# A gather kernel: loading a third block of one batch's rows ahead, in four pieces issued between ScalarE's zeroing copies

**Chip, cores, metric.** One core of a Trainium2 chip. The metric is the time of one execution on the device in microseconds (us); lower is better. Times are medians. A ratio is the mean time of one kernel's fast runs over the mean of the other's fast runs of the same rounds, so it is not quite the ratio of the medians quoted. A run is called fast or slow by how far it lies from the fastest of the same kernel.

## The reference

```python
# x: (32, 512, 1024) float32; indices: (32, 128) int32 in 0..511, drawn with a fixed seed
for b in range(batch):
    result[b] = x[b, indices[b]]          # (128, 1024) per batch
```

It is a gather of 128 rows of 4 KB from each of 32 batches. Among 128 draws from 512 rows there are repeats: a batch names 109 to 120 distinct rows. The kernel uses that.

## The kernel before

Batches 0 to 4 (the HEAD) are gathered straight by their index columns, repeats included. For every later batch the kernel works out which positions are the first to name a row, gathers only those rows into one of eight ring buffers `u` (places that are not needed get an index out of bounds and are skipped: in the profile of this kernel the gather queue moved 15.01 MB, where 32 x 128 whole rows would be 16.78), and then spreads the rows to all 128 positions with a 0/1 matrix on TensorE. ScalarE copies the product from PSUM, and SyncE stores the block. The ring buffers are zeroed once by ScalarE, so that a skipped place holds zeros.

Batch 5 (HALF) is treated specially: rows 0 to 255 of it are loaded as two plain blocks at the start, before any index is known, and only its rows from 256 up are gathered. These are the parts concerned, with cuts marked:

```python
early = [rows.tile([N, D], F32, name=f"early{k}") for k in range(2)]
for k in range(2):                                    # ScalarE's DMA queue
    load = act(nc.scalar.dma_start, out=early[k][:], in_=xf[HALF * S + k * N:HALF * S + (k + 1) * N])
# ... indices transposed; then the head:
for b in range(HEAD):
    gather(blocks[b], ..., b)                         # GpSimd, indirect DMA
    store(b)                                          # SyncE, 512 KB to DRAM
# ... in step0 of batch 5's group: a row below 2N counts as already present
#         scalar=2.0 * N, in1=cnt[:, c], op0=ALU.is_lt, op1=ALU.add
held = []
for k in range(RING):
    u = ring.tile([N, D], F32, name=f"u{k}")
    act(nc.scalar.copy, out=u[:], in_=zero[:].to_broadcast([N, D]))
    held.append(u)
# ... half_rows(h, last=False): product of the early blocks, kept open in PSUM
#         for k in range(2):
#             pe(mm, ps[:], lhsT=spread[HALF, "early"][k], rhs=early[k][:, w], start=k == 0, stop=False)
step0(0); step0(1)
for g in range(AHEAD):                                # groups of three batches
    step1(g)                                          # TensorE, VectorE: place of each row
    if 0 < g < AHEAD - 1: step0(g + 1)
    step2(g)                                          # the rows to gather and the spread matrix
    for b in of_group(g):
        if b < HEAD + RING: fetch(b)                  # GpSimd gathers into the ring
    if g == 0: half_spread()
    elif g < 3: half_rows(g - 1, False)
for b in range(HEAD, B):
    spread_rows(b); fetch(b + RING)                   # product, copy, store; next gather
    # ... steps of a later group
```

On TensorE the early products of batch 5 stand between the steps that yield the addresses of groups 1, 2 and 3: the gathers of a later group are not issued before TensorE has come through the products ahead of their step.

Of the kernel before, what the change touches and what calls it, by code (L numbers as in the profile page):

```python
# [6 lines left out]
F32 = mybir.dt.float32  # L7
# [21 lines left out]
def kernel(ctx, tc, x, indices, out):  # L29
# [16 lines left out]
    nc = tc.nc  # L46
    B, S, D = x.shape
    N = indices.shape[1]
    HEAD, RING, GROUP, AHEAD, FAR = 5, 8, 3, 4, 1024
    HALF = HEAD  # L50
    PAIRED = range(12, 20)
    GROUPS = (B - HEAD) // GROUP
    assert 2 * N <= S <= FAR and (B - HEAD) % GROUP == 0
    const = ctx.enter_context(tc.tile_pool(name="const", bufs=1))
    ring = ctx.enter_context(tc.tile_pool(name="ring", bufs=1))
    rows = ctx.enter_context(tc.tile_pool(name="rows", bufs=1))
    pick = ctx.enter_context(tc.tile_pool(name="pick", bufs=1))
# [5 lines left out]
    pe, dve, act = InOrder(tc), InOrder(tc), InOrder(tc)  # L63
    mm, v = nc.tensor.matmul, nc.vector
# [12 lines left out]
    for p0, p1, at0 in ((0, 36, 0), (36, 48, 112), (48, 104, 36), (104, 108, 124), (108, N, 92)):  # L77
# [16 lines left out]
        in_=vals[:].bitcast(I32).rearrange("p (n two) -> p n two", two=2)[:, :, 0])  # L94
# [2 lines left out]


    xf = x.flatten_outer_dims()
    early = [rows.tile([N, D], F32, name=f"early{k}") for k in range(2)]  # L100
    for k in range(2):
        load = act(nc.scalar.dma_start, out=early[k][:], in_=xf[HALF * S + k * N:HALF * S + (k + 1) * N])
        if k == 0:
# [9 lines left out]
    idxF = const.tile([N, B], F32, name="idxF")  # L113
# [14 lines left out]
    for b in range(B):  # L128
        if b not in PAIRED:
            blocks[b] = rows.tile([N, D], F32, name=f"block{b}")[:]  # L130
# [5 lines left out]
    def store(b):  # L136
        if b not in PAIRED:
            nc.sync.dma_start(out=of[b * N:(b + 1) * N], in_=blocks[b])
        elif b % 2:
            nc.sync.dma_start(out=of[(b - 1) * N:(b + 1) * N].rearrange("(t p) d -> p t d", t=2),  # L140
                              in_=blocks[b - 1, "pair"][:])
# [5 lines left out]
    def table(name, dtype):  # L147
        return const.tile([N, B], dtype, name=name)

    cnt, lead, slot = table("cnt", F32), table("lead", F16), table("slot", F16)  # L150
# [4 lines left out]
    bcs, packs, spread = {}, {}, {}  # L155

    def of_group(g):
        return range(HEAD + g * GROUP, HEAD + (g + 1) * GROUP)

    def cols(t, g):  # L160
        return t[:, HEAD + g * GROUP:HEAD + (g + 1) * GROUP]
# [4 lines left out]
    def step0(g):  # L166

        bcs[g] = bc = pbc.tile([N, 4, N], F32, name="bc")
        for k, b in enumerate(of_group(g)):
            pe(mm, bc[:, k], lhsT=ident[:, b:b + 1].to_broadcast([N, N]), rhs=vf[:], start=True, stop=True)  # L170
        for k, b in enumerate(of_group(g)):
            junk = junkp.tile([N, N], F16, name="junk")
            dve(v.scalar_tensor_tensor, out=junk[:], in0=bc[:, k], scalar=idxF[:, b:b + 1], in1=below[:],
                op0=ALU.is_equal, op1=ALU.mult, accum_out=cnt[:, b:b + 1])
        if HALF in of_group(g):
            c = slice(HALF, HALF + 1)
            dve(v.scalar_tensor_tensor, out=cnt[:, c], in0=idxF[:, c], scalar=2.0 * N, in1=cnt[:, c],
                op0=ALU.is_lt, op1=ALU.add)
        dve(v.tensor_scalar, out=cols(lead, g), in0=cols(cnt, g), scalar1=0.0, scalar2=None, op0=ALU.is_equal)
        for b in of_group(g):  # L180
            if b < B - 2:
                dve(v.tensor_tensor, out=past[:, b + 1:b + 2], in0=past[:, b:b + 1], in1=lead[:, b:b + 1], op=ALU.add)
# [33 lines left out]
    for k in range(RING):  # L216
        u = ring.tile([N, D], F32, name=f"u{k}")
        act(nc.scalar.copy, out=u[:], in_=zero[:].to_broadcast([N, D]))
        held.append(u)

    def half_spread():

        same = pick.tile([N, 2, N], F32, name="same")
        for k in range(2):
            dve(v.tensor_scalar, out=same[:, k], in0=bcs[0][:, HALF - HEAD], scalar1=less[:], scalar2=float(k * N),
                op0=ALU.add, op1=ALU.is_equal)
        spread[HALF, "early"] = [same[:, k] for k in range(2)]

    def half_rows(h, last):
        w = slice(h * 512, (h + 1) * 512)  # L230
        if not last:
            spread[HALF, h] = pout.tile([N, 512], F32, name="ps")
        ps = spread[HALF, h]
        if last:
            pe(mm, ps[:], lhsT=spread[HALF], rhs=held[(HALF - HEAD) % RING][:, w], start=False, stop=True)
        else:
            for k in range(2):
                pe(mm, ps[:], lhsT=spread[HALF, "early"][k], rhs=early[k][:, w], start=k == 0, stop=False)
        if last:
            nc.scalar.copy(out=blocks[HALF][:, w], in_=ps[:])  # L240

    def spread_rows(b):
        for h in range(2):
            if b == HALF:
                half_rows(h, True)
                continue
            w = slice(h * 512, (h + 1) * 512)
            ps = pout.tile([N, 512], F32, name="ps")
            pe(mm, ps[:], lhsT=spread[b], rhs=held[(b - HEAD) % RING][:, w], start=True, stop=True)
            nc.scalar.copy(out=blocks[b][:, w], in_=ps[:])  # L250
        store(b)

    step0(0)
    step0(1)
    for g in range(AHEAD):
        step1(g)
        if 0 < g < AHEAD - 1:
            step0(g + 1)
        step2(g)
        for b in of_group(g):  # L260
            if b < HEAD + RING:
                fetch(b)
        if g == 0:
            half_spread()
        elif g < 3:
            half_rows(g - 1, False)
# [36 lines left out]
```

## Time and profile before

| | before |
|---|---|
| median, first 3 runs | 87.41 us (87.28 to 87.68) |
| span on the core | 85.6 us |
| DMA busy share 12 to 82 us | 1.02 to 1.03 |
| rate in that time | about 418 GB/s |
| moved in all | 32.91 MB |

The shares come from the table of busy times by stretches. A share a little above 1 is what this profile shows for full engines. The prediction below shows the lines and reads them.

### The profile page before, as it was taken

How to read it: one execution, taken by the hardware profiler on the slowest of the kernel's cores; microseconds unless marked ns; L12 is line 12 of the kernel's file. 1: busy time of each engine (PE TensorE's matmuls, PEld its weight loads, DVE VectorE, ACT ScalarE, POOL GpSimd, SP SyncE). 2: the span in 40 equal slices, each digit the busy share in tenths (PEclk: the TensorE clock that was granted, in tenths of full speed). 3: DMA queues.
4: the chain of work that ended last, by engine and by line, in shares of the span. 5: the costliest groups of instructions: out<-in, count | busy, mean ns of one | idle time of the engine just before them, and what ended most of it. 6: DMA issues, size and time to landing. Idle time of an engine off the chain costs nothing.

```text
span 85.6 us, 827 instructions
## 1 busy us (share of the span) xinstructions
PE 61.3 (72%) x189; PEld 25.3 (29%) x189; DVE 31.6 (37%) x160; ACT 40.5 (47%) x63; POOL 33.3 (39%) x43
## 2 busy tenths in 40 slices
PE   0320379576999999999878987878789888889300
PEld 0300242323434444444333433322223333323000
DVE  4498793786563864844641453000000000000000
ACT  0899930000665665555554354455544554446400
POOL 6587578727444455554332444443320000000000
PEclk9999999999999999999999999999999999999996
DMA  0799999999999999999999999999999999999980
GB/s 1 274 375 344 302 342 415 415 417 417 419 419 419 417 421 419 415 419 417 419 419 419 417 419 413 421 413 423 417 417 419 419 419 419 423 415 417 423 337 15
DMA packets 9636, 32.91 MB, mean 384 GB/s; under 512 B 1584, under 2 KB 1616, under 8 KB 9632
## 3 DMA queue, kind: packets, MB, share of 16 engines
q1 hardware_dynamic: 4736, 16.81, 48.2%
q0 software_dynamic: 4608, 15.01, 44.7%
q10 hardware_dynamic: 288, 1.05, 3.3%
q8 instruction: 1, 0.02, 0.1%
q14 instruction: 3, 0.02, 0.1%
HBM read 17.86 MB, written 16.78 MB: 404 GB/s over the span
## 4 chain that ended last, share of the span: by engine, by line
DMA 40%; PE 21%; issue 14%; DVE 14%; POOL 3%; ACT 1%; SPq 0%; POOLq 0%; DVEq 0%
DMA u<-in_x_dram,at 37%; PE ps L24 20%; DVE junk L24 3%; POOL u L121 3%; DVE pack L24 3%; DMA vals<-in_indices_dram 2%; DVE past L24 2%; DVE nth L24 2%; DVE s L24 1%; PE pos L24 1%; DVE slot L24 1%; ACT block L250 1%; DVE lead L24 1%; DVE same L24 1%; SPq L68 0%
## 5 line engine op out<-in xcount | busy, mean ns | idle before, releaser
L24 PE MATMUL ps<-u,s 128*128 128x512 f32 x108 | 52.4, 611 | 6.8 <-DMA u<-in_x_dram,at 6.2
L121 POOL DMA_INDIRECT u<-in_x_dram,at x27 | 26.9, 997 | 26.7 <-PE ps L24 5.8
L250 ACT COPY block<-ps 128x512 f32<-128x512 f32 x36 | 21.1, 585 | 18.7 <-PE ps L24 17.6
L24 PEld LDWEIGHTS ps<-u,s 128*128 128x128 f32 x108 | 18.3, 189 | 29.1 <-ACT block L250 14.8
L250 ACT COPY pair<-ps 128x512 f32<-128x512 f32 x16 | 9.4, 585 | 8.7 <-PE ps L24 7.1
L24 DVE SCALAR_TENSOR_TENSOR junk<-bc,idxF,below 128x128 f16<-128x128 f32 x27 | 8.0, 347 | 7.1 <-PE bc L24 7.1
L24 ACT COPY u<-zero 128x1024 f32<-128x1024 f32 x8 | 7.7, 1040 | 0.0
L24 PE MATMUL pos<-near,pack 128*128 128x1 f16 x27 | 2.0, 167 | 5.6 <-DVE pack L24 5.6
L240 ACT COPY block<-ps 128x512 f32<-128x512 f32 x2 | 1.2, 585 | 10.1 <-PE ps L24 10.1
L24 PE MATMUL ps<-early,same 128*128 128x512 f32 x8 | 5.7, 854 | 0.0
L24 DVE TENSOR_TENSOR pack<-turn,slot 128x384 f16<-128x384 f16 (+2 forms) x10 | 5.1, 518 | 0.3
L24 DVE TENSOR_TENSOR s<-bc,at 128x384 f32<-128x384 f32 x9 | 5.0, 558 | 0.3
L24 PEld LDWEIGHTS <-pack 128*128 128x128 f16 x27 | 1.7, 99 | 9.5 <-DVE pack L24 7.4
L24 DVE TENSOR_TENSOR past<-past,lead 128x1 f16<-128x1 f16 x25 | 4.1, 163 | 0.9
L24 PE MATMUL bc<-vf,ident 128*128 128x128 f16 x27 | 3.4, 256 | 1.3 <-DVE same L24 1.3
L121 POOL DMA_INDIRECT block<-in_x_dram,idxT x4 | 3.8, 947 | 1.3 <-issue 0.9
L24 PEld LDWEIGHTS <-ident 128*128 128x128 f16 x27 | 2.4, 111 | 4.2 <-issue 4.2
L24 DVE TENSOR_SCALAR at<-pos 128x3 int32<-128x3 f32 x9 | 1.4, 160 | 5.1 <-PE pos L24 4.8
L24 DVE CAST nth<-rk 128x3 int32<-128x3 f32 x9 | 1.4, 160 | 3.7 <-PE rk L24 3.3
L21 PE MATMUL pos<-ident,vf 128*128 128x32 f16 x1 | 0.2, 210 | 3.6 <-DVE vf L24 3.6
L24 ACT ACT_TABLE_LOAD x1 | 1.3, 1283 | 2.5 <-DVE vf L24 2.5
L24 PEld LDWEIGHTS ps<-early,same 128*128 128x128 f32 x8 | 1.9, 257 | 1.5 <-issue 1.5
(32 smaller groups left out, 18.4 us busy)
## 6 DMA issues: line engine op xcount, KB each, us to landing
out_dram<-block SPq DMA_DIRECT2D x24, 512.0 KB, 8.0
out_dram<-pair SPq DMA_DIRECT2D x4, 1024.0 KB, 11.1
early<-in_x_dram ACTq DMA_DIRECT2D x2, 512.0 KB, 3.8
u<-in_x_dram,at POOLq DMA_INDIRECT x27, 15.2
block<-in_x_dram,idxT POOLq DMA_INDIRECT x4, 6.4
vals<-in_indices_dram SPq DMA_DIRECT2D x1, 32.0 KB, 2.0
first<-in_indices_dram SPq DMA_DIRECT2D x1, 1.0 KB, 1.8
block<-in_x_dram,first POOLq DMA_INDIRECT x1, 5.2
```

The lines of the kernel that those rows point to most:

```text
L21: self.last = do(*args, **kw)
L24: self.last = do(*args, **kw)
L121: nc.gpsimd.indirect_dma_start(out=dst, out_offset=None, in_=xf[:], in_offset=bass.IndirectOffsetOnAxis(ap=at, axis=0), element_offset=b * ...
L240: nc.scalar.copy(out=blocks[HALF][:, w], in_=ps[:])
L250: nc.scalar.copy(out=blocks[b][:, w], in_=ps[:])
```

## The change

The intent: between about 5 and 12 us the kernel moves less than 418 GB/s (328 in the mean), and ScalarE has little to do but zero the ring. So a third block, rows 256 to 383 of batch 5, is loaded as four pieces of 32 rows, issued from ScalarE's queue between its copies, and the gather of batch 5 then fetches only rows from 384 up. The core of the diff (the other hunks raise 2 to EARLY = 3 in the comparison, the spread matrices and the early products):

```diff
+    EARLY, PIECES = 3, 4
@@
-    early = [rows.tile([N, D], F32, name=f"early{k}") for k in range(2)]
+    early = [rows.tile([N, D], F32, name=f"early{k}") for k in range(EARLY)]
@@
-            dve(v.scalar_tensor_tensor, out=cnt[:, c], in0=idxF[:, c], scalar=2.0 * N, in1=cnt[:, c],
+            dve(v.scalar_tensor_tensor, out=cnt[:, c], in0=idxF[:, c], scalar=float(EARLY * N), in1=cnt[:, c],
@@
         act(nc.scalar.copy, out=u[:], in_=zero[:].to_broadcast([N, D]))
         held.append(u)
+        if 0 < k <= PIECES:
+            w = slice((k - 1) * N // PIECES, k * N // PIECES)
+            at0 = HALF * S + (EARLY - 1) * N
+            act(nc.scalar.dma_start, out=early[EARLY - 1][w], in_=xf[at0 + w.start:at0 + w.stop])
@@
-            for k in range(2):
+            for k in range(EARLY):
                 pe(mm, ps[:], lhsT=spread[HALF, "early"][k], rhs=early[k][:, w], start=k == 0, stop=False)
```

More of the change, by code (lines that the diff above doesn't have):

```diff
@@ L50 @@
     HALF = HEAD
+    EARLY, PIECES = 3, 4
     PAIRED = range(12, 20)
     GROUPS = (B - HEAD) // GROUP
-    assert 2 * N <= S <= FAR and (B - HEAD) % GROUP == 0
+    assert EARLY * N <= S <= FAR and (B - HEAD) % GROUP == 0
     const = ctx.enter_context(tc.tile_pool(name="const", bufs=1))
@@ L219 @@
         held.append(u)
+        if 0 < k <= PIECES:
+            w = slice((k - 1) * N // PIECES, k * N // PIECES)
+            at0 = HALF * S + (EARLY - 1) * N
+            act(nc.scalar.dma_start, out=early[EARLY - 1][w], in_=xf[at0 + w.start:at0 + w.stop])
     def half_spread():
-        same = pick.tile([N, 2, N], F32, name="same")
-        for k in range(2):
+        same = pick.tile([N, EARLY, N], F32, name="same")
+        for k in range(EARLY):
             dve(v.tensor_scalar, out=same[:, k], in0=bcs[0][:, HALF - HEAD], scalar1=less[:], scalar2=float(k * N),
                 op0=ALU.add, op1=ALU.is_equal)
-        spread[HALF, "early"] = [same[:, k] for k in range(2)]
+        spread[HALF, "early"] = [same[:, k] for k in range(EARLY)]
     def half_rows(h, last):
@@ L236, in half_rows @@
         else:
-            for k in range(2):
+            for k in range(EARLY):
                 pe(mm, ps[:], lhsT=spread[HALF, "early"][k], rhs=early[k][:, w], start=k == 0, stop=False)
```

## The prediction

> **What bounds the kernel now.** I began with the page's 40 slices, to see which resource is full and from when to when. The span is 85.6 us, so a slice is 2.14 us.
>
> ```profile
> PE   0320379576999999999878987878789888889300
> ACT  0899930000665665555554354455544554446400
> DMA  0799999999999999999999999999999999999980
> GB/s 1 274 375 344 302 342 415 415 417 417 419 419 419 417 421 419 415 419 417 419 419 419 417 419 413 421 413 423 417 417 419 419 419 419 423 415 417 423 337 15
> ```
>
> The DMA row is at 9 from the third slice to the last but two, and from about 12 us on the rate stands at 415 to 423 GB/s whatever the other engines do. The kernel is bound by DMA; the exception is the rate between slices 4 and 6 (302 to 344), which is what the change aims at. The question is whether the engines are idle there or only slow, so next I read the table by stretches. Its last two columns are the DMA busy share (1.03 is what a full stage shows) and GB/s.
>
> ```profile
> core 0: us, PE busy (x) PEld busy (x) DVE busy (x) ACT busy (x) POOL busy (x), PEclk, DMA share, GB/s
> 4.00:6.00 2.00, 0.75 (x7) 0.39 (x4) 1.86 (x17) 2.00 (x3) 1.39 (x2) 1.00 1.01 381
> 8.00:10.00 2.00, 0.30 (x5) 0.24 (x6) 1.59 (x6) 2.00 (x3) 0.98 (x2) 1.00 1.03 336
> 10.00:12.00 2.00, 1.07 (x7) 0.79 (x7) 1.90 (x11) 1.47 (x2) 1.70 (x2) 1.00 0.93 274
> 24.00:30.00 6.00, 6.00 (x24) 2.74 (x22) 3.49 (x17) 3.77 (x7) 3.01 (x4) 1.00 1.03 419
> ```
>
> The dip is mostly not idleness. From 8 to 10 us the engines are as busy (1.03) as in the steady stage and still move only 336 GB/s. Only 10 to 12 us shows room: 0.93 against 1.03, that is 0.10 x 2 us = 0.2 us of all engines. The DMA view by stretches says what is slow. These are the queue lines for 4 to 6 us (q10 is ScalarE's queue, carrying the early loads), for 8 to 10 us, for 10 to 12 us, and for 24 to 26 us; q0 is GpSimd's gather queue.
>
> ```profile
> q10 hardware_dynamic: 181, 0.61, 79.9%
> ...
> q0 software_dynamic: 189, 0.67, 103.2%
> ...
> q0 software_dynamic: 134, 0.50, 86.8%
> ...
> q0 software_dynamic: 251, 0.83, 102.3%
> ```
>
> A row is one 4096-byte packet, so share x 2 us x 16 engines over (MB / 4096) is the engine time of a row: q10 at 4 to 6 us 25.6 us / 149 = 172 ns; q0 at 8 to 10 us 33.0 / 164 = 201 ns; at 10 to 12 us 27.8 / 122 = 228 ns; at 24 to 26 us 32.7 / 203 = 161 ns. The four indirect gathers of whole index columns (batches 1 to 4) have slow packets; later gathers of distinct rows do not, even with the queue alone. The profile does not say why. ScalarE's zeroing copies (3.81 to 11.47 us) run at the same time, but q10's rows are only a little slow beside them.
>
> [...]two queues together give 419 GB/s (24 to 30 us), one gather queue alone 0.83 MB in 2 us, 415. [...]This trace has no DMA issued behind a copy, so it is only my inference that the pieces may be issued well ahead of the copies that they stand between. [...]the first four early matmuls take 3.76 us, the next four 1.96.
>
> **The change part by part.** *Transfers.* Added: 128 rows, 128 x 172 ns / 16 = 1.38 us of all engines, using the cost of a row in the early loads. Removed: the gather of batch 5 skips rows below 384 instead of 256. The inputs have a fixed seed, so I counted: batch 5 has 60 distinct rows from 256 up and 27 from 384 up, so 33 rows fall away, 33 x 161 / 16 = 0.33 us. Net +1.05 us of engine time, +95 rows or 0.39 MB (0.93 us at 418 GB/s). Against it stands the room of 0.2 us at 10 to 12 us: +0.85 us. *ScalarE.* Four issues; the two loads of today cost 0.38 and 0.46 us of its sequencer.
>
> ```profile
> 1.61 0.38 ACTq L21 DMA_DIRECT2D early<-in_x_dram  x1
> 2.02 0.46 ACTq L24 DMA_DIRECT2D early<-in_x_dram  x1
> 3.81 7.66 ACT L24 COPY u<-zero 128x1024 f32<-128x1024 f32 x8
> ...
> 11.50 3.76 PE L24 MATMUL ps<-early,same 128*128 128x512 f32 x4
> ...
> 16.67 1.96 PE L24 MATMUL ps<-early,same 128*128 128x512 f32 x4
> ```
>
> If issue blocks the copies they end 4 x 0.42 = 1.7 us later, at 13.2 us; ScalarE is idle until 21.25 us and the last zeroed buffer is gathered into at 20.27 us. Free either way. *VectorE.* One more comparison in half_spread: the two take 0.52 us, so +0.26 us. *TensorE.* Each half gets a third product, two instructions: 2 x 0.94 = 1.9 us at most at 11.5 us[...], and 2 x 0.49 = 1.0 us at 16.67 us. The first product of batch 5's gathered rows, now at 20.11 us, starts 0.26 + 1.0 to 1.9 + 1.0 = 2.3 to 3.2 us later, and so do its store and the next gather (22.34 us). That lies beside DMA work: gathers issued from 20 to 22 us land 12.5 us later, so the queue holds far more than 3 us. From 24 to 26 us q0 alone already kept the engines full without a store. So TensorE's delay costs nothing at the end; what counts is the bytes.
>
> **The rivals.** (1) *The load fills the dip and is free:* then only the 0.33 us removed shows, 87.1 us. For it: 302 to 344 GB/s against 418 looks like 0.6 MB of room. Against it: busy shares of 1.01 to 1.03 in that dip. A middle form is likelier: if the slow packets belong to the time up to 12 us rather than to those four gathers, pushing gathers past 12 us makes some rows cost 161 instead of 228 ns; 1.3 us moved at that ratio returns about 0.4 us, 87.9 us. (2) *TensorE becomes the bound around 20 to 28 us:* it works without a pause there (6.00 of 6.00 us), and 3 us more could empty the gather queue. Against it: the 12.5 us to landing. If it did, 1 to 2 us would be lost, about 89.5 us. (3) *The third product waits for a late piece* at about 15 us. Gathers and loads seem served in order of issue (the first store, issued at 7.97 us, has no packet before 11 us), so a piece issued at 7 us could land at 12 to 13. A wait would be under 2 us and is hidden for the reason of (2).
>
> **Range and chances.** Main case 87.41 + 0.85 = 88.26. I take off a little for the middle form of (1): 88.2 us. Low 87.5 is nearly full absorption; high 88.7 is the net 1.05 us with nothing absorbed and 0.25 us for a small starvation. A verdict of slower needs over 89.16 us and so (2): 0.04. Faster needs under 85.66 us, which nothing gives: 0.01.
>
> **What would show it.** Right: bytes up by 0.39 MB; rate back at 415 to 420 about 1 us later; a last gather landing about 0.8 us later; the products of batch 5 starting 2 to 3 us later with the DMA share still 1.03 from 16 to 30 us. Wrong: GB/s rising towards 400 between 5 and 12 us (absorption, rival 1), or a share below 1.0 between 20 and 32 us (rival 2). What would mislead me most is the cause of the slow packets, which I do not know.

Marked cuts stand where the prediction told of hardware what no trace of this case shows. They take no term out of its sum, which is 87.41 + 1.38 - 0.33 - 0.20 = 88.26 us; that a piece of 32 rows is spread over the engines as the early loads are was the author's assumption. The 1.0 in "1.0 to 1.9" is 2 x 0.49 us, as if the third product at 11.5 us took the time of those at 16.67 us. Why the first four early products took 0.94 us each and the next four 0.49 was not shown.

## The result

The changed kernel takes **96.91 us** (95.64 to 97.68, 6 runs) against 87.55 us (87.08 to 88.76, 6 runs) for the kernel before. The ratio of the fast runs is **1.105** (95% interval 1.095 to 1.114). The span grew from 85.6 to 95.4 us. The prediction of 88.2 us was far off.

The profiled execution of the changed kernel counts as slow (97.18 us, 1.6% over the fastest). I took it once more later (97.24 us), and it showed the same picture. No profile of the changed kernel at its fast times exists; but its four fast runs are 9.1 us longer than the kernel before (96.50 against 87.36 us in the mean), and the profile of e7 below, a fast run, has the same hole in the DMA row (0.02 and 0.00 from 28 to 32 us).

First the slices of the page of the changed kernel, in the rows that the prediction showed of the kernel before. A slice is now 2.385 us.

```profile
PE   0311197002789499999999999999987888875000
ACT  0996000470000045656565656676664444444000
DMA  0899999999941836999999999999999999999990
GB/s 10 262 328 304 366 381 409 423 419 412 419 165 22 259 124 197 299 388 416 412 414 426 409 407 419 424 414 417 421 422 414 423 419 423 412 422 424 414 397 26
```

The loss has a place. The DMA row, full before from the third slice on, now falls to 4, 1, 8, 3, 6 in the twelfth to sixteenth slice, and the rate to 165, 22, 259, 124 and 197. TensorE has a hole of its own earlier (slices eight and nine), and ScalarE one earlier still (slices five to seven). After 40 us DMA is full again (1.02, 412 GB/s from 40 to 60 us). The table by stretches gives the size (its last two columns are DMA share and GB/s); here the kernel before:

```profile
26.00:40.00 14.00, 13.63 (x48) 6.04 (x48) 7.62 (x35) 8.54 (x15) 7.17 (x8) 1.00 1.03 419
```

and the changed kernel:

```profile
24.00:26.00 2.00, 1.55 (x7) 0.45 (x5) 0.61 (x4) 0.00 (x0) 0.00 (x0) 1.00 1.04 424
28.00:30.00 2.00, 2.00 (x3) 0.67 (x2) 0.68 (x3) 0.00 (x0) 1.00 (x1) 1.00 0.00 0
...
26.00:40.00 14.00, 12.20 (x37) 5.29 (x38) 7.66 (x35) 3.52 (x6) 4.59 (x5) 1.00 0.54 172
```

Up to 26 us DMA is full. From 26 to 40 us it moves 172 GB/s instead of 419, so (1 - 172/419) x 14 us = 8.3 us of full-rate transfer are lost, and from 28 to 30 us it moves nothing. The bytes added, 33.30 - 32.91 = 0.39 MB, are 0.9 us at 418 GB/s. Together 9.2 us of the 9.8 us by which the span grew.

Why did DMA run dry? Backwards: gathers were not issued. The timeline of GpSimd in the changed kernel (start, duration, what, and in brackets the idle time before it):

```profile
19.29 1.00 POOL L122 DMA_INDIRECT u<-in_x_dram,at  x1 [2.42 <-ACT u L24]
28.89 1.00 POOL L122 DMA_INDIRECT u<-in_x_dram,at  x1 [8.60 <-issue]
30.19 1.00 POOL L122 DMA_INDIRECT u<-in_x_dram,at  x1 [0.30 <-issue]
35.59 1.00 POOL L122 DMA_INDIRECT u<-in_x_dram,at  x1 [4.39 <-PE bc L24]
```

The second and the last of these are the gathers into the seventh ring buffer and into the first one that comes free. In the kernel before they stand here:

```profile
18.97 1.00 POOL L121 DMA_INDIRECT u<-in_x_dram,at  x1 [1.50 <-issue]
22.34 1.00 POOL L121 DMA_INDIRECT u<-in_x_dram,at  x1 [1.07 <-PE bc L24]
```

So they are 9.9 and 13.3 us late. Their addresses come from steps that TensorE runs behind the early products. The timeline of TensorE in the changed kernel shows those, and its waits name what the first of them waited for:

```profile
23.14 2.04 PE L24 MATMUL ps<-early,same 128*128 128x512 f32 x2 [7.14 <-DMA early<-in_x_dram]
...
26.61 5.33 PE L24 MATMUL ps<-early,same 128*128 128x512 f32 x6
```

TensorE stood 7.14 us in front of the third product, for a piece of the third block. Then the products of the second half took 5.33 us for six instructions, 0.89 us each, where the kernel before needed 0.49 (four in 1.96 us at 16.67 us, in the prediction's lines). And the piece was late because of this, in the timeline of ScalarE of the changed kernel (ACTq is the issue of a DMA by ScalarE's sequencer):

```profile
2.60 1.31 ACTq L24 DMA_DIRECT2D early<-in_x_dram  x2
3.81 3.88 ACT L24 COPY u<-zero 128x1024 f32<-128x1024 f32 x4
6.90 0.32 ACTq L24 DMA_DIRECT2D early<-in_x_dram  x1
7.60 1.04 ACT L24 COPY u<-zero 128x1024 f32<-128x1024 f32 x1
17.62 0.32 ACTq L24 DMA_DIRECT2D early<-in_x_dram  x1
17.98 2.94 ACT L24 COPY u<-zero 128x1024 f32<-128x1024 f32 x3 [9.34 <-issue]
```

Two pieces went out at once, the third at 6.90 us, and the **fourth only at 17.62 us**. ScalarE, in order, did nothing from 8.64 us on; its last three zeroing copies came 9 us later. The piece then landed at 22.89 us by the chain of waits. "issue" means that this profile saw nothing that released it. But the trace records, for each DMA, the semaphores on which its issue waits and the one that its landing raises. For the four pieces in the changed kernel they say (read from the records, not a view of the profile; the numbers are those of the trace):

```
early2 piece 1   issued  2.60 us   waits on nothing         raises 117
early2 piece 2   issued  3.59 us   waits on 102             raises 102   (raised before by the load of the indices, to 3.57 us)
early2 piece 3   issued  6.90 us   waits on 113             raises 113   (raised before by the second early load, to 6.88 us)
early2 piece 4   issued 17.62 us   waits on 115             raises 115   (raised before by the store of batch 0; records of it to 16.94 us)
```

So the second and the third piece were issued 0.02 us after the last record of the landing of another DMA, and the fourth waited for the landing of the store of batch 0 (14 records of that landing are in the trace, where the store of batch 1 has 16). In the data the two have nothing to do with each other. My reading was that the order in which the framework's scheduler lays out the DMAs of SyncE and ScalarE decides which of them share a semaphore, and that the first stores had come ahead of pieces in that order. No view shows that rule; e1, e2 and e7 are built on it. The store was issued at 10.10 us, behind gathers that fill the DMA engines (share 1.03 from 10 to 26 us), and showed its first packets after 14 us.

This was a reading. The experiments, e1 to e10 (none is called e5), had to show that the wait, and not the bytes or the third user of the DMA engines, is the cost.

### The profile page after: what moved, and what is told of

The parts are those of the page before. It is cut to its first block, busy times and chain, and to the rows that moved or that the text cites. A ratio compares the mean times of both kernels' runs of the same rounds, so it can differ in the third digit from the quotient of the medians.

```text
span 95.4 us, 843 instructions
## 1 busy us (share of the span) xinstructions
PE 64.7 (68%) x193; PEld 26.9 (28%) x193; DVE 31.9 (33%) x161; ACT 40.7 (43%) x63; POOL 33.7 (35%) x43
## 2 busy tenths in 40 slices
DMA packets 9828, 33.30 MB, mean 349 GB/s; under 512 B 1681, under 2 KB 1713, under 8 KB 9824
## 4 chain that ended last, share of the span: by engine, by line
PE 36%; DMA 25%; issue 15%; POOL 6%; ACT 5%; DVE 2%; POOLq 1%; SPq 0%; ACTq 0%
PE ps L24 34%; DMA u<-in_x_dram,at 17%; POOL u L122 6%; DMA early<-in_x_dram 6%; ACT u L24 5%; DMA vals<-in_indices_dram 2%; DVE pack L24 1%; PE bc L24 1%; DVE nth L24 1%; PE pos L24 1%; ACT block L255 1%; SPq L69 0%; DVE slot L24 0%; ACTq L24 0%; PE rk L24 0%
## 5 line engine op out<-in xcount | busy, mean ns | idle before, releaser
L24 PE MATMUL ps<-u,s 128*128 128x512 f32 x108 | 50.9, 608 | 2.9 <-DMA u<-in_x_dram,at 2.9
L24 PE MATMUL ps<-early,same 128*128 128x512 f32 x12 | 11.1, 1084 | 7.1 <-DMA early<-in_x_dram 7.1
L24 PEld LDWEIGHTS ps<-early,same 128*128 128x128 f32 x12 | 3.5, 324 | 11.8 <-issue 11.8
```

The source lines that it names most:

```text
L24: self.last = do(*args, **kw)
```

## The experiments

The theories, as named in the expectations: **W**, the wait for the store's landing holds the fourth piece, the piece holds TensorE, TensorE holds the gathers. **R1**, the transfer itself, its bytes or its 32-row pieces beside the other queues, slows DMA. **R2**, the stalled ScalarE costs, through the late zeroing copies that the gathers into the ring have to wait for. All runs gave the right result, except the one marked.

### Pieces as they are, without the wait for the store (e1_stores_after)

```diff
     for b in range(HEAD):
         gather(blocks[b], ..., b)
-        store(b)
@@ after the loop of zeroing copies and pieces
+    for b in range(HEAD):
+        tc.add_manual_dep(store(b).ins, piece.ins.name,
+                          mybir.DependencyInfo(mybir.DependencyClass.NoSync, mybir.DependencyReason.DATA), reason=...)
```

The dependency is one of order in the scheduler, without a wait; ScalarE's list is the same instruction for instruction. That the pieces are then issued without a stall is what the timeline below has to show.

> Same pieces at the same places in ScalarE's order; only the five first stores are queued by the scheduler behind the pieces, so that the fourth piece no longer shares a semaphore with the store of batch 0. Theory W (the semaphore wait holds the fourth piece, the piece holds TensorE's third product, and that holds the gathers): all four pieces issue before 5 us, no TensorE wait for a piece over 1 us, DMA share at or above 1.0 from 14 to 80 us, time 88.2 us (87.6 to 88.9). Rival R1 (the extra transfer or its 32-row pieces slow the DMA queues): still 95 to 97 us. Rival R2 (late zeroing copies): also 88, since the copies are no longer late; told apart by e3 and e4.

Measured: 88.73 us (88.56 to 89.04), ratio 1.015 (1.010 to 1.021). Of the 9.4 us of loss 1.1 us are left. The timeline of ScalarE in this run:

```profile
2.60 1.06 ACTq L24 DMA_DIRECT2D early<-in_x_dram  x2
3.81 1.05 ACT L24 COPY u<-zero 128x1024 f32<-128x1024 f32 x1
3.82 0.79 ACTq L24 DMA_DIRECT2D early<-in_x_dram  x2
4.76 6.71 ACT L24 COPY u<-zero 128x1024 f32<-128x1024 f32 x7
```

All four pieces are out by 4.61 us, ahead of the copies between which they stand in the program, and the copies end at 11.47 us as in the kernel before. DMA from 26 to 40 us in this run:

```profile
26.00:40.00 14.00, 14.00 (x49) 6.19 (x48) 8.77 (x44) 8.55 (x15) 7.51 (x8) 1.00 1.03 418
```

R1 falls: the same bytes in the same pieces cost 1.5%. W stands; R2 isn't tested by this, since the copies are in time again.

### Two pieces of 64 rows (e2_two_pieces)

```diff
-    EARLY, PIECES = 3, 4
+    EARLY, PIECES = 3, 2
```

> Two pieces of 64 rows in place of four of 32; the same bytes[...]. W: both pieces issue before 5 us, 88.2 us (87.6 to 88.9). R1 (bytes): 95 to 97 us.

Measured: 89.30 us (88.76 to 89.55), ratio 1.021 (1.014 to 1.027), a little above what I expected and with an interval that overlaps that of e1. The loss is gone here too, by a way that leaves the scheduling of the stores alone: both pieces were issued between 2.60 and 3.76 us, and the copies ran from 3.81 to 11.47 us without a stall.

### The wait kept, the third product moved (e3_product_late)

```diff
         if last:
+            pe(mm, ps[:], lhsT=spread[HALF, "early"][EARLY - 1], rhs=early[EARLY - 1][:, w], start=False, stop=False)
             pe(mm, ps[:], lhsT=spread[HALF], rhs=held[...][:, w], start=False, stop=True)
         else:
-            for k in range(EARLY):
+            for k in range(EARLY - 1):
```

> The change as it is, with the wait, but the third product is moved from the early stage to the last stage of batch 5, behind the gathers of groups 1 to 3 in TensorE's order. W: the fourth piece still issues near 17.6 us and ScalarE still stands for 9 us, but TensorE no longer waits in the early stage; the gathers into u6 and u7 issue by about 22 us instead of 28.9, DMA does not run dry, 88 to 90 us. R2 (the late zeroing copies are what costs): 94 us or more.

Measured: 88.79 us (88.31 to 91.64, one run slow), ratio 1.014 (1.007 to 1.021). ScalarE's timeline still has the stall, and here the profile names what ended it:

```profile
17.30 0.32 ACTq L24 DMA_DIRECT2D early<-in_x_dram  x1
17.66 2.93 ACT L24 COPY u<-zero 128x1024 f32<-128x1024 f32 x3 [9.03 <-DMA out_dram<-block]
```

A copy that zeroes a buffer was released by a store's landing, through the DMA issue ahead of it in ScalarE's list. Yet the time is that of e1. The gathers into the last three ring buffers were issued at 18.97, 20.27 and 21.57 us; in the changed kernel the last two of them came at 28.89 and 30.19 us. So R2 falls: a ScalarE that stands for 9 us costs nothing measurable here. What cost the time is that TensorE waited for the piece ahead of the steps that feed the gathers; with the product behind those steps TensorE waits 0.25 us for it:

```profile
22.90 1.10 PE L24 MATMUL ps<-early,same 128*128 128x512 f32 x2 [0.25 <-DMA early<-in_x_dram]
```

### The pieces as loads that nobody reads (e4_unused_loads)

```diff
# the kernel before, with
+        if 0 < k <= 4:
+            w = slice((k - 1) * 32, k * 32)
+            at0 = HALF * S + 2 * N
+            act(nc.scalar.dma_start, out=spare[w], in_=xf[at0 + w.start:at0 + w.stop])
```

> The kernel before plus four 32-row loads at the places of the pieces, into a tile that nobody reads; same waits on ScalarE's queue as in the change, no product, no rows saved. W: ScalarE's queue stands until about 17 us, TensorE does not; only bytes are paid: 0.52 MB, that is 88.4 to 89.0 us. R2: 94 us or more. R1: 94 us or more.

Measured: 88.82 us (88.54 to 89.69), ratio 1.018 (1.010 to 1.026). The fourth load was again issued at 17.30 us, with the same 9.03 us of idle ScalarE. This agrees with e3, and it gives the price of the load alone: 0.0177 x 87.4 us = 1.5 us (0.9 to 2.2), where my working had 1.38.

### The wait without the bytes (e6_wait_only)

```diff
# the kernel before, with tick = a tile of 128 x 64, and
+        if 0 < k <= 4:
+            act(nc.scalar.dma_start, out=tick[w], in_=xf[at0 + w.start:at0 + w.stop, 0:64])
@@ half_spread: a third matrix that is never true (all zeros)
@@ half_rows, early stage
+            pe(mm, ps[:, 0:64], lhsT=spread[HALF, "early"][2], rhs=tick[:], start=False, stop=False)
```

> The kernel before plus the waits without the bytes: four loads of 32 rows x 256 bytes at the places of the pieces (0.03 MB instead of 0.52), and a third product of 64 columns by a mask of zeros that needs them; the result stays right, no rows are saved. The fourth load shares a semaphore with the store of batch 0, which lands at about 15.3 us in the kernel before (17.6 in the changed one). W: TensorE waits some 4 to 5 us for the fourth load, the gathers into u6 and u7 and the products of batch 5 come 5 to 8 us late, and what exceeds the queue's stock of about 5 us is lost: 88.5 to 91 us. R1 (bytes or pieces are the cost): 87.4 us.

Measured: 93.14 us (three fast runs 92.72 to 93.14, two slow at 96.11 and 96.48), ratio of the fast runs 1.062 (1.051 to 1.073), so about 5.4 us lost with 0.03 MB added. So waiting without the bytes costs more than half of the change's loss (9.1 us by the same measure), and more than I expected (88.5 to 91); the added product is no rival, as e10 shows. The profile fell on a slow run, so I take from it only the order of events: the fourth load issued at 16.35 us, a wait of TensorE that did not exist before,

```profile
22.35 0.66 PE L24 MATMUL ps<-tick,same 128*128 128x64 f32 x2 [6.68 <-DMA tick<-in_x_dram]
```

and DMA shares of 0.10 at 26 to 28 us and 0.08 at 32 to 34 us. The fourth load, of 8 KB, was issued at 16.35 and let TensorE go on only at 22.35 us. I had counted on a wait of 4 to 5 us. (The stock of about 5 us in the expectation is my estimate from the changed kernel, explained under "Why the prediction was wrong".)

### The wait made longer (e7_wait_later)

```diff
             at0 = HALF * S + (EARLY - 1) * N
+            if k == PIECES:
+                act(nc.scalar.dma_start, out=spare[:], in_=xf[at0:at0 + 32, 0:64])
```

The extra load is meant to take over the wait for the store of batch 0, and to leave the fourth piece one for the store of batch 1.

> The change plus one tiny load (32 rows x 256 bytes) ahead of the fourth piece, so that the fourth piece shares its semaphore with the store of batch 1 instead of batch 0. Dose: that store lands about 2 us later. W: the fourth piece issues at 19 to 20 us instead of 17.6, the time goes up by about the same, 98 to 100 us. R1: 96.9 us, unchanged.

Measured: 99.20 us (97.90 to 99.50), ratio 1.126 (1.112 to 1.141), against 1.105 for the change: 0.022 x 87.4 = 1.9 us more. The two intervals just overlap (1.112 and 1.114), so the size of that is rough. The piece's issue moved by as much, and TensorE's wait from 7.14 to 9.06 us:

```profile
18.04 0.32 ACTq L24 DMA_DIRECT2D spare<-in_x_dram  x1
19.60 0.32 ACTq L24 DMA_DIRECT2D early<-in_x_dram  x1
...
25.08 2.05 PE L24 MATMUL ps<-early,same 128*128 128x512 f32 x2 [9.06 <-DMA early<-in_x_dram]
```

17.62 to 19.60 us is 2.0 us, and the profile names a store's landing as what released the copies behind the piece, after 11.32 us. This agrees with W: the stock of issued gathers was used up, and the later piece cost its delay in full (1.9 us for 2.0).

### The saving alone (e8_saving_only, wrong)

```diff
-            dve(..., scalar=2.0 * N, in1=cnt[:, c], op0=ALU.is_lt, op1=ALU.add)
+            dve(..., scalar=3.0 * N, in1=cnt[:, c], op0=ALU.is_lt, op1=ALU.add)
```

> The kernel before with only the comparison changed: batch 5's rows 256 to 383 are not gathered (33 rows, 0.135 MB), and nothing is loaded in their place, so batch 5 is wrong on purpose. My working: 33 x 161 ns / 16 = 0.33 us less, ratio 0.996. If skipped rows cost as much as fetched ones: ratio 1.000.

Measured: 87.44 us, ratio 0.999 (0.991 to 1.006). My 0.996 lies within the interval, and so does no saving. Inconclusive, save that the 33 rows are worth at most 0.8 us.

### The compute alone (e10_product_only)

```diff
# the kernel before, with a third comparison that is never true, and
-            for k in range(2):
-                pe(mm, ps[:], lhsT=spread[HALF, "early"][k], rhs=early[k][:, w], start=k == 0, stop=False)
+            for k in range(3):
+                pe(mm, ps[:], lhsT=spread[HALF, "early"][k], rhs=early[min(k, 1)][:, w], start=k == 0, stop=False)
```

> The kernel before plus the compute of the change alone: a third comparison (never true) and a third product per half, by that mask of zeros over the second early block; no load, no piece, no saved row; the result stays right. Products of batch 5 start 2.3 to 3.2 us later than 20.1 us. My step 'TensorE's delay costs nothing at the end': ratio 1.000 (0.995 to 1.005), DMA share still 1.03 from 16 to 40 us. If that step is wrong by itself: 1.01 or more.

Measured: 87.75 us, ratio 1.002 (0.997 to 1.007). The first product of batch 5's gathered rows started at 21.87 us instead of 20.11, and the gather into the first free ring buffer at 24.10 instead of 22.34: 1.8 us late, and DMA from 16 to 40 us stayed full. A delay of that size is indeed hidden.

### The opposite: one block (e9_one_block)

```diff
-    for k in range(2):       # early loads, comparison, matrices, products: all from 2 to 1
+    for k in range(1):
```

> The opposite of the change: one block of 128 rows of batch 5 loaded ahead, not two; rows from 128 up are gathered. If the DMA engines have no spare time after 4 us, every extra row costs and this gains: 128 rows less at 165 to 172 ns / 16 = 1.3 to 1.4 us saved, distinct rows of 128 to 255 added (about 28, 0.28 us), and an idle gap of about 0.4 us before the gather of batch 1 arrives: 86.8 us (86.3 to 87.3). If the second load fills time that would stand idle: 87.4 us or more.

Measured: 88.62 us (87.93 to 88.92), ratio 1.013 (1.006 to 1.020): slower, against my main expectation and in line with the other that I had named. In this run DMA is far from full at the start:

```profile
4.00:6.00 2.00, 0.75 (x7) 0.39 (x4) 1.86 (x17) 2.00 (x3) 1.38 (x2) 1.00 0.75 190
```

So the second block does fill time that would stand idle (0.75 against 1.01 in the kernel before). It is not this stretch alone: from 6 to 8 and from 8 to 10 us the shares are 0.86 and 0.82, against 1.01 and 1.03. Together (0.26 + 0.15 + 0.21) x 2 = 1.2 us of all engines, more than the 1.0 us (0.41 MB at 418 GB/s) that the smaller load saves. The third block finds no such room. Two blocks are the best of the three.

### The changed kernel again (after_again)

> The changed kernel once more, unaltered, because its first profiled execution was counted as slow (1.6% over its fastest). If the reading holds in the fast state: time 95.6 to 97 us, the fourth piece again issued at 16 to 19 us, TensorE waiting 6 to 8 us for it, DMA standing still for several us between 26 and 38 us.

Measured: 97.24 us in one run, of unknown state by itself (1.7% over the fastest of the six). Fourth piece at 17.76 us, TensorE's wait 7.4 us, DMA share 0.01 from 28 to 30 us, and the copies behind the piece now with the releaser named:

```profile
18.12 2.93 ACT L24 COPY u<-zero 128x1024 f32<-128x1024 f32 x3 [9.31 <-DMA out_dram<-block]
```

No version among these beats the kernel before, and none of the readings points to one: with the wait gone, the third block is a cost of bytes.

## Why the prediction was wrong

*DMA is the bound, and the dip from 5 to 12 us is slow, not idle.* Right. e1 and e4 pay for the bytes. My sum for the transfer was +0.85 us; e1, the change without the wait, measures 0.015 x 87.4 = 1.35 us (0.9 to 1.8), so the 0.2 us of room that I set against it did not show. Rival 1, free filling, is refuted by the same run, and so is its middle form (87.9 us, 0.5 us more).

*ScalarE: "If issue blocks the copies they end 4 x 0.42 = 1.7 us later ... Free either way."* **This is the step that failed.** I counted the durations of the issues and the order of the copies, and took it that a DMA with a fresh destination waits for nothing. The copies ended 9 us later (20.92 us against 11.47), because the issue of the fourth piece waited 9 us for a store's landing. That ScalarE stood was in itself indeed free, as e3 and e4 show.

*Rival 3: the third product waits for a late piece; "A wait would be under 2 us and is hidden".* The right place, the wrong size, for the reason above: the wait was 7.14 us, and the piece was issued at 17.62 us, not at 7. The copies' pace doesn't set the issue: my inference that the sequencer issues pieces ahead of the copies was right (e1: all four by 4.61 us), and what held the fourth was not the copies.

*"TensorE's delay costs nothing at the end".* Right for the 2 to 3 us it was worked out for (e10: 1.002). It is a statement about a stock and not about TensorE. The queue of issued gathers covered a delay of 1.8 us (e10); in the changed kernel, where it had run out, a further delay of 2.0 us cost 1.9 (e7). In the changed kernel the first reuse of a ring buffer came 13.3 us late and 8.3 us of transfer were lost, so the stock was worth about 5 us there, an estimate. e3 agrees: there that gather is not in the timeline up to 26 us, so it came over 3.6 us late (22.34 us in the kernel before), and DMA stayed full (1.00 to 1.07 in every stretch from 14 to 40 us). I had written "far more than 3 us" from the 12.5 us to landing of a gather. That figure counts stores and gathers together, and the stores stop as well when TensorE stops (from 26 to 36 us the changed kernel's store queue shows 1 packet, the gather queue 452).

*Rival 2: TensorE empties the gather queue, "about 89.5 us".* This is what happened, and my sign for it, a DMA share below 1.0 between 20 and 32 us, came (0.60 and 0.00 from 26 to 30 us), but with the delay from a wait instead of from work, and with an addition that I didn't foresee: after the wait the products took 0.89 us instead of 0.49 each, 6 x 0.40 = 2.4 us more. The traces do not say why. The granted clock does not settle it: the profile of the changed kernel shows 1.00 from 26 to 32 us beside these durations, that of its repetition 0.50 from 24 to 32 us. That the pause of 7.14 us is the cause is not shown either: in e3 four products took 3.63 us from 17.47 us without a pause over 1 us since 12.2 us, and no run separates the share of the longer products in the loss from the wait's.

What the wait did to the copies can be read from the trace: those behind the fourth piece began at 17.98 us, 0.36 us after its issue began, where in the kernel before they had ended at 11.47 us.

What stays open: why rows cost up to 228 ns between 6 and 12 us. Changed and unchanged kernels all have a slow stretch there, at somewhat different times. The zeroing copies alone don't explain it: in the changed kernel ScalarE's copies from 18 to 21 us ran beside a full 414 to 422 GB/s. I made no experiment on it.

## What to carry to other kernels

The fourth piece brought not only its bytes (1.5 us for all four in e4) and its issue time (0.32 us) but also a wait for another DMA's landing, which held it until 17.62 us and cost 8.2 us (e1 against the change: 88.73 against 96.91 us). So ahead of such a change, look in the compiled program for what each new DMA waits on, and when that lands. An instruction on an engine that is "free" can hold a critical one: ScalarE had nothing else to do, and yet TensorE waited 7.14 us for the piece that ScalarE was to issue. With the product moved behind the steps that feed the gathers the wait was 0.25 us (e3), so put the consumer of an uncertain load as late as it can stand. And a delay was hidden here by a stock with an end (1.8 us were free in e10, 13.3 us cost 8.3 us of transfer in the change): estimate the stock in us before calling a delay free.
